# Attention and recurrence served from two queues, chunk 1's norms at a higher rate, output banks copied first

## The chip, the cores and the metric

The kernel runs on one core of a Trainium2 chip. The metric is the device time of one launch in microseconds (us), median of several runs. TensorE (PE) does the products, VectorE (DVE), ScalarE (ACT) and GpSimd (POOL) the rest, and SyncE (SP) issues the DMA transfers from one queue, in order.

## The reference

One layer of a decoder trunk on 1024 prompt rows and 64 sample rows (8 sequences of 8), 1024 wide:

```python
x = x + 0.5 * rms_norm(swiglu(rms_norm(x, norm_ffn1_pre), ffn1_w_gu, ffn1_w_down), norm_ffn1_post)
h = rms_norm(x, norm_mix_pre)
z = h @ w_in + b_in
q, k, v, hq, hf, hi, hg = jnp.split(z, ...)
a = rms_norm(window_attention(q, k, v, attn_sinks), attn_out_norm)   # 128 back, learned sinks
f = lb + (1 - lb) * sigmoid(hf)
o, S = hgrn2_chunked(silu(hq), 1 - f, log(f), hi, s0)                # gated linear recurrence
o = rms_norm(o, hg_out_norm) * silu(hg)
x = x + rms_norm(concat([a, o]) @ w_out, norm_mix_post)
x = x + 0.5 * rms_norm(swiglu(rms_norm(x, norm_ffn2_pre), ffn2_w_gu, ffn2_w_down), norm_ffn2_post)
```

The feed-forward layers are 2816 wide inside. Keys, values and states are returned too.

## The kernel before

**Chunks.** The rows are cut into three chunks: chunk 0 has two blocks of 128 prompt rows and the 64 sample rows (320 columns), chunks 1 and 2 have three blocks each (384 columns). Every fp32 matrix is split into a high and a low part (`split`, L254 to L256: ACT casts the high part, DVE or POOL subtracts it for the low one), and every product is done as three (`mm3`, L276 to L280). The feed-forward layers treat chunk 0 plainly (`up0`, `down`) and chunks 1 and 2 together by seven products of sums of halves; the down part of that is `pair` (L925), whose argument names products by key, as (5,3), (7,), (4,). A product of `pair` takes eleven 128-row slices in six groups (five of two slices, one of one). For each group SP loads the weights (`raw<-fb`, L880) and the activations (`ar<-fa`, L892, into a slot of the tag h384, 8 slots), and they are split; the activations are fetched one group ahead. The products go to three PSUM banks, which `put` (L901) adds to the sums after the last group (L905).

**The middle of the layer** (L1573 to L1603) is where the change is. In program order: `w_in_units(0)`, the projection of chunk 0; products (5,3), (7,) and (4,) of the first feed-forward layer, which belong to chunks 1 and 2; `w_in_units(1)`; `w_out_units(0)`; `w_in_units(2)`; the first five units of the second feed-forward layer for chunk 0 (`f2.head`, each unit two banks of 24 products); `w_out_units(1)`; nine more units; `w_out_units(2)`. For chunks 1 and 2 `w_out_units` is done twice, for each half of the columns, in three banks of 128x512.

**Side work.** Small work is written as generators and woven into the products. `stream(name, gen, rate)` (L95) enters one; each `tick()` (L98), called once to twice per weight tile, advances every stream by its rate in steps; `need(name)` (L108) runs what is left of one to its end there. Streams of norms are `half`, `c0`, `c1` and `c2`: `half_n` (L407) squares a half and multiplies it by the gain, `post_n` (L416) loads the residual (`xt`, L424), adds it (L426) and stores the sum (`x1N`, L427), `pre_n` (L430) scales, transposes on TensorE (L454), and splits (L459) into the tiles `h` that `w_in_units` reads. `done1` and `half1` enter these at the rate `RA1` = 0.75, `done_mix` at `RB0` and `RB1`. The stream `m0`, `m1` or `m2` is the mixer of a chunk: `mixer(n)` (L1449) alternates one step of attention (`attn_block`, L1110, ten steps a block) with one of the recurrence (`hgrn_block`, L1265, twelve steps a block). For chunk 0 it has sample attention (L1299), the output of keys and values, and the sample recurrence (L1378) as well. It is entered when all of the chunk's projection is written, and drained by `need` ahead of the chunk's `w_out`.

Within a recurrence block, `intra` (L1184) makes a 64-row causal product by halving: at each level TensorE does small products `lv` (L1204) or `l` (L1228), after which DVE and POOL multiply their operands for the next one (L1239, L1241). In attention, `sc` are the scores, `pT` the transposed weights (L1165), `pv` the weighted values (L1176).

The order of the instructions on each engine is fixed when the program is built, by a scheduler that weighs readiness against program order. Each engine then works through its own row and waits at an instruction whose operands aren't there. Slots of a pool (`t2` 8, `h384` 8, `big` 12, `wsp` 8, `raw` 3, PSUM `mm` 4 and `ax` 4) tie a later request to the last reader of an earlier one.

**Output banks.** At the end of a half of `w_out_units(1)` and `(2)`, ACT squares each of the three banks for the norm (L1495), and DVE multiplies it by the gain into SBUF (L1496). The bank is free after both.

Of the kernel before, what the change touches and what calls it, by code (L numbers as in the profile page):

```python
# [13 lines left out]
AF = mybir.ActivationFunctionType  # L14
# [29 lines left out]
def tile_step(ctx: ExitStack, tc: tile.TileContext, A: dict, O: list):  # L44
# [53 lines left out]
    def tick():  # L98
        for name in list(streams):
            st = streams[name]  # L100
            st[2] += st[1]
            while st[2] >= 1.0:
                st[2] -= 1.0
                if next(st[0], "end") == "end":
                    del streams[name]
                    break

    def need(name):  # L108
# [860 lines left out]
    def mixing(tp, h):  # L969
# [27 lines left out]

        def w_in_units(n):
            w = WIDTH[n]
# [31 lines left out]
            for m in range(1, 4):  # L1031
                tr(m, z["q"][:, m, :w])
            z["k"] = big()
            for a in range(4):
# [400 lines left out]

        def both(*gens):
            gens = list(gens)
            while gens:
                for g_ in list(gens):
                    if next(g_, "end") == "end":  # L1440
                        gens.remove(g_)
                    else:
                        yield

        def chain(*gens):
            for g_ in gens:
                yield from g_

        def mixer(n):  # L1449
            MT[n] = new_h(n)  # L1450
            at = [attn_block(n, b) for b in range(NPB[n])]
            hg = [hgrn_block(n, b) for b in range(NPB[n])]
            if n == 0:
                at = at + [sample_attn(), kv_out(0)]
                hg = hg + [sample_hgrn()]
            if n == 2:
                at.append(kv_out(2))
            yield from both(chain(*hg), chain(*at))
            if n == 2:
                nc.sync.dma_start(O[4][0, 0].rearrange("h k v -> k h v"), state[0])  # L1460

# [9 lines left out]
        def w_out_units(n, ys, sums):  # L1471
# [14 lines left out]
            for hf in range(2):  # L1486
# [7 lines left out]
                for i in range(3):  # L1494
                    S.activation(junk, banks[i], AF.Square, accum_out=sm[:, 0, 4 * hf + i:4 * hf + i + 1])  # L1495
                    V.tensor_tensor(y[hf][:, i], banks[i], g, op=ALU.mult)  # L1496

        return w_in_units, mixer, w_out_units


# [3 lines left out]

    RM = [0.95, 1.0, 1.3]
    RA0, RA1, RB0, RB1 = 1.2, 0.75, 0.6, 0.8
    HEAD1, HEAD2 = 6, (5, 14, 22)
# [64 lines left out]

    with tc.tile_pool(name="mx", bufs=1) as tp:  # L1573
        w_in_units, mixer, w_out_units = mixing(tp, hmix)
        need("c0")
        w_in_units(0)
        stream("m0", mixer(0), RM[0])
        half1(1)
# [120 lines left out]
```

## Time and profile before

| | us |
|---|---|
| median of 3 runs | 2049.44 |
| lowest, highest | 2048.64, 2050.24 |
| span of the profiled execution | 2045.3 |
| TensorE busy in it | 2006.7 |

The profiled execution's own time beside its span isn't given apart from the three runs; the median is 4.1 us above the span. A row of the windows view gives, for one stretch of the span, the busy time and the count of instructions on each engine, then the clock that TensorE was granted (1.00 is full). A row of the timeline gives start, duration, engine, line, operation, tiles and shape, and in brackets the idle time before it with what ended it.

### The profile page before, as it was taken

The numbers are of one execution on the slowest core, as the hardware profiler recorded it, in microseconds if no ns is written. First come the engines' busy times: TensorE is split into PE (matmuls) and PEld (weight loads), VectorE is DVE, ScalarE is ACT, GpSimd is POOL, SyncE is SP. The second block draws the span as 40 slices with busy tenths as digits, with TensorE's granted clock in tenths as the row PEclk, the third lists the DMA queues.
The fourth block names the chain that finished last, engine by engine and source line by source line (L and its number), as shares of the span: only waits on it lengthen the run. The fifth ranks groups of instructions, "written<-read, shape, count | busy, mean of one in ns | idle before, by whom it ended". The sixth has DMA issues, their size and how long they took to land.

```text
span 2045.3 us, 34828 instructions
## 1 busy us (share of the span) xinstructions
PE 2006.7 (98%) x13273; PEld 1856.7 (91%) x13273; DVE 1452.6 (71%) x2493; ACT 933.5 (46%) x1679; POOL 550.1 (27%) x508
## 2 busy tenths in 40 slices
PE   9999999999999999899999998999999999999998
PEld 8999999999998987697898897878999999999886
DVE  5776667885568557777678756766889888655667
ACT  6534333444455445435344444544544444444552
POOL 0013433654113101311113310210046554510201
PEclk9999999999999999799999998999999999999999
DMA  8455445556777545556434243525565556576874
GB/s 254 140 158 169 139 156 164 200 182 219 238 235 213 159 149 171 160 145 184 127 96 138 87 141 94 163 87 184 168 193 200 191 188 209 195 241 222 289 257 136
DMA packets 372368, 360.09 MB, mean 176 GB/s; under 512 B 40590, under 2 KB 294361, under 8 KB 372185
## 3 DMA queue, kind: packets, MB, share of 16 engines
q1 hardware_dynamic: 371401, 356.42, 55.2%
q8 instruction: 104, 1.70, 0.3%
q10 hardware_dynamic: 800, 1.44, 0.2%
q14 instruction: 63, 0.52, 0.1%
HBM read 279.85 MB, written 78.94 MB: 175 GB/s over the span
## 4 chain that ended last, share of the span: by engine, by line
PE 91%; DVE 3%; DMA 3%; ACT 1%; issue 1%; SPq 0%; DVEq 0%; ACTq 0%
PE mm L278 27%; PE mm L279 26%; PE mm L280 26%; PE c L280 1%; PE c L278 1%; PE c L279 1%; PE sc L1127 1%; DMA ar<-fa 1%; PE pv L1176 1%; DMA raw<-in_ffn_w_gu_dram 1%; PE lv L1204 1%; PE pT L1165 1%; PE tr L497 1%; DVE w L256 1%; DMA xt<-in_x_prompt_dram 0%
## 5 line engine op out<-in xcount | busy, mean ns | idle before, releaser
L278 PE MATMUL mm<-h,wsph 128*128 128x320 f32 (+1 forms) x1296 | 414.7, 322 | 3.7 <-ACT sg L632 2.2
L279 PE MATMUL mm<-h,wsph 128*128 128x320 f32 (+1 forms) x1296 | 412.5, 319 | 0.0
L280 PE MATMUL mm<-h,wspl 128*128 128x320 f32 (+1 forms) x1296 | 411.7, 318 | 0.0
L255 ACT CAST wsph<-raw 128x1024 fp32r<-128x1024 f32 x202 | 211.3, 1048 | 293.9 <-PE mm L279 237.1
L256 DVE TENSOR_TENSOR wspl<-raw,wsph 128x1024 fp32r<-128x1024 f32 x202 | 251.0, 1245 | 119.3 <-ACT wsph L255 118.5
L256 DVE TENSOR_TENSOR w<-raw,w 128x512 fp32r<-128x512 f32 (+1 forms) x226 | 250.0, 1110 | 84.9 <-ACT w L255 82.8
L255 ACT CAST w<-raw 128x512 fp32r<-128x512 f32 (+1 forms) x226 | 169.6, 754 | 207.3 <-PE mm L279 109.8
L278 PEld LDWEIGHTS mm<-h,wsph 128*128 128x128 f32 x1296 | 244.6, 189 | 11.0 <-issue 3.1
L280 PEld LDWEIGHTS mm<-h,wspl 128*128 128x128 f32 x1296 | 244.7, 189 | 4.0 <-issue 3.5
L279 PEld LDWEIGHTS mm<-h,wsph 128*128 128x128 f32 x1296 | 245.0, 189 | 3.2 <-issue 2.6
L278 PE MATMUL mm<-h,w 128*128 128x384 f32 x704 | 235.8, 335 | 1.2 <-DVE big L725 1.2
L279 PE MATMUL mm<-h,w 128*128 128x384 f32 x704 | 235.8, 335 | 0.0
L280 PE MATMUL mm<-h,w 128*128 128x384 f32 x704 | 230.5, 335 | 0.0
L279 PE MATMUL mm<-w,h 128*128 128x512 f32 x462 | 181.6, 393 | 0.0
L278 PE MATMUL mm<-w,h 128*128 128x512 f32 x462 | 180.8, 395 | 0.5 <-DVE big L905 0.5
L280 PE MATMUL mm<-w,h 128*128 128x512 f32 x462 | 179.5, 392 | 0.0
L280 PE MATMUL mm<-big,w 128*128 128x384 f32 x528 | 176.8, 335 | 1.5 <-DVE w L256 1.5
L279 PE MATMUL mm<-big,w 128*128 128x384 f32 x528 | 176.7, 335 | 0.0
L278 PE MATMUL mm<-big,w 128*128 128x384 f32 x528 | 176.6, 335 | 0.0
L709 POOL TENSOR_TENSOR big<-big 128x384 f32<-128x384 f32 x88 | 111.7, 1269 | 236.5 <-ACT big L722 116.2
L256 DVE TENSOR_TENSOR w<-t,w 128x512 fp32r<-128x512 f32 x176 | 160.5, 922 | 17.5 <-ACT w L255 17.0
L278 PEld LDWEIGHTS mm<-h,w 128*128 128x128 f32 x704 | 132.2, 188 | 1.6 <-DVE big L725 1.6
(359 smaller groups left out, 3881.2 us busy)
## 6 DMA issues: line engine op xcount, KB each, us to landing
raw<-in_ffn_w_gu_dram SPq DMA_DIRECT2D x156, 512.0 KB
raw<-in_ffn_w_down_dram SPq DMA_DIRECT2D x74, 512.0 KB
raw<-in_w_in_dram SPq DMA_DIRECT2D x54, 512.0 KB
ar<-fa SPq DMA_DIRECT2D x70, 384.0 KB
big<-in_ffn_w_down_dram SPq DMA_DIRECT2D x88, 256.0 KB
fb<-big SPq DMA_DIRECT2D x44, 512.0 KB
raw<-fb SPq DMA_DIRECT2D x40, 512.0 KB
fa<-big SPq DMA_DIRECT2D x22, 768.0 KB
```

The source lines that it names most:

```text
L255: S.copy(hi, src)
L256: (lo_eng or V).tensor_tensor(lo, src, hi.bitcast(F32), op=ALU.subtract)
L278: PE.matmul(out, a[0], b[0], start=first, stop=False, skip_group_check=resume)
L279: PE.matmul(out, a[0], b[1], start=False, stop=False, skip_group_check=resume)
L280: PE.matmul(out, a[1], b[0], start=False, stop=last, skip_group_check=resume)
L497: PE.transpose(bank[:, i * P:(i + 1) * P], y[kh][:, i, k * P:(k + 1) * P], ident)
L709: G.tensor_tensor(e[:, i], e[:, i], e[:, i + 1], op=ALU.mult)
L1127: PE.matmul(banks[g][:, i * 256:i * 256 + wk], zq[64 * g:64 * g + 64, 2 * pr + i, b * P:(b + 1) * P], kx[64 * g:64 * g + 64, k0:k0 + wk], ...
L1165: PE.transpose(bank[:, (i * nk + kb) * P:(i * nk + kb + 1) * P], pt[g][:, i, kb * P:(kb + 1) * P], ident)
L1176: PE.matmul(ob[64 * g:64 * g + 64, pr * 256:pr * 256 + 256], vn[:, vb, g * 64:g * 64 + 64], pT[g][:, :2 * wk].rearrange("p (i k t) -> p k ...
L1204: PE.matmul(b4[cs, a, :32], x[:, a, cs], y[:, a, cs], start=True, stop=True)
```

## The change

1. `mixer`, `both` and `chain` go. Two queues, `at` (attention) and `hg` (recurrence), are entered as streams that never end ahead of `w_in_units(0)`, at 0.45 and 0.65 steps a tick. In each `w_in_units(n)`, `ready("at", n)` appends the chunk's attention blocks when the queries are projected, and `ready("hg", n)` its recurrence blocks when the recurrence's values are. Before, the whole mixer waited for the end of the projection, and advanced 0.95, 1.0 and 1.3 steps a tick for chunks 0, 1 and 2.
2. Ahead of `w_out_units(n)`, `need_mix(n)` runs what is left of chunks up to n, one step of each queue in turn.
3. `RA1`, the rate of `half`, `c1` and `c2`, goes from 0.75 to 1.2.
4. In `w_out_units`, ACT copies the three banks to SBUF first; then ACT squares the copies, and POOL multiplies them by the gain.

```diff
+    queues = {"at": [], "hg": []}
+
+    def steps(name):
+        q = queues[name]
+        while True:
+            while q:
+                if next(q[0][1], "end") == "end":
+                    q.pop(0)
+                else:
+                    break
+            yield
+
+    def need_mix(n):
+        gens = {k: streams[k][0] for k in queues}
+        while any(q and q[0][0] <= n for q in queues.values()):
+            for k, q in queues.items():
+                if q and q[0][0] <= n:
+                    next(gens[k])
...
             for m in range(1, 4):
                 tr(m, z["q"][:, m, :w])
+            ready("at", n)
...
                 V.tensor_tensor(hv[:r, i], banks[i][:r], bhi[:r], op=ALU.add)
+            ready("hg", n)
...
-        def mixer(n):
-            MT[n] = new_h(n)
-            at = [attn_block(n, b) for b in range(NPB[n])]
-            hg = [hgrn_block(n, b) for b in range(NPB[n])]
-            if n == 0:
-                at = at + [sample_attn(), kv_out(0)]
-                hg = hg + [sample_hgrn()]
-            if n == 2:
-                at.append(kv_out(2))
-            yield from both(chain(*hg), chain(*at))
...
+        def ready(kind, n):
+            if n not in MT:
+                MT[n] = new_h(n)
+            if kind == "at":
+                gens = [attn_block(n, b) for b in range(NPB[n])]
+                if n == 0:
+                    gens += [sample_attn(), kv_out(0)]
+                if n == 2:
+                    gens.append(kv_out(2))
+            else:
+                gens = [hgrn_block(n, b) for b in range(NPB[n])]
+                if n == 0:
+                    gens.append(sample_hgrn())
+                if n == 2:
+                    gens.append(state_out())
+            queues[kind] += [(n, g) for g in gens]
...
                 for i in range(3):
-                    S.activation(junk, banks[i], AF.Square, accum_out=sm[:, 0, 4 * hf + i:4 * hf + i + 1])
-                    V.tensor_tensor(y[hf][:, i], banks[i], g, op=ALU.mult)
+                    S.copy(y[hf][:, i], banks[i])
+                for i in range(3):
+                    S.activation(junk, y[hf][:, i], AF.Square, accum_out=sm[:, 0, 4 * hf + i:4 * hf + i + 1])
+                    G.tensor_tensor(y[hf][:, i], y[hf][:, i], g, op=ALU.mult)
...
-    RM = [0.95, 1.0, 1.3]
-    RA0, RA1, RB0, RB1 = 1.2, 0.75, 0.6, 0.8
+    RAT, RHG = 0.45, 0.65
+    RA0, RA1, RB0, RB1 = 1.2, 1.2, 0.6, 0.8
...
         need("c0")
+        stream("at", steps("at"), RAT)
+        stream("hg", steps("hg"), RHG)
         w_in_units(0)
-        stream("m0", mixer(0), RM[0])
         half1(1)
...
         w_in_units(1)
-        need("m0")
-        stream("m1", mixer(1), RM[1])
+        need_mix(0)
         w_out_units(0, ym, sums)
...
         f2.head(range(HEAD2[0]))
-        need("m1")
-        stream("m2", mixer(2), RM[2])
+        need_mix(1)
         w_out_units(1, ym, sums)
...
-        need("m2")
+        need_mix(2)
+        streams.pop("at"), streams.pop("hg")
         w_out_units(2, ym, sums)
```

Two places show how the order of the instructions moves. Line numbers of the changed kernel are 19 to 21 higher.

**The loads of key (4,).** This is SP's row before, from the third of the six activation loads (`ar<-fa`) on. The other names are the weights of the product (`raw<-fb`), chunk 1's gain row (`gb`), residual (`xt`) and sums (`x1N`), and weights of the next projection.

```order
L892 DMA ar_8348<-fa_114 128x2x384
L880 DMA raw_8275<-fb_115 128x2x512
L892 DMA ar_8398<-fa_114 128x2x384
L880 DMA raw_8341<-fb_115 128x2x512
L892 DMA ar_8451<-fa_114 128x2x384
L880 DMA raw_8391<-fb_115 128x2x512
L400 DMA gb_7894<-in_norm_ffn_post_dram 128x512
L880 DMA raw_8444<-fb_115 128x512
L424 DMA xt_8092<-in_x_prompt_dram 128x512
L424 DMA xt_8096<-in_x_prompt_dram 128x512
L262 DMA raw_8661<-in_w_in_dram 128x8x128
L427 DMA x1N_96<-big_5759 128x512
```

Five of the six loads stand ahead of chunk 1's norm, the sixth behind it. And this is SP's row of the changed kernel, from the last stores of that norm on; `osc` is an output of sample attention.

```order
L446 DMA x1N_96<-big_5759 128x512
L443 DMA xt_8421<-in_x_prompt_dram 128x512
L446 DMA x1N_96<-big_6059 128x512
L443 DMA xt_8425<-in_x_prompt_dram 128x512
L446 DMA x1N_96<-big_5759 128x512
L446 DMA x1N_96<-big_6059 128x512
L1388 DMA osc<-t_1207_8540 128x64
L911 DMA ar_8636<-fa_114 128x2x384
L419 DMA gb_8688<-in_norm_ffn_post_dram 128x512
L911 DMA ar_8722<-fa_114 128x2x384
L911 DMA ar_8778<-fa_114 128x2x384
```

`ar_8636` is the second load; the first, `ar_8556`, stands 28 rows ahead of it and ahead of the norm. So the second to sixth loads are behind the norm now. On DVE, 80 rows stand between the eviction of key (7,)'s last bank (`big_6060<-mm_8193`, L924) and the split of `ar_8636`. On TensorE, 116 small products stand between the first group and the second, whose first product is the last row here; `tr` are the transposes of chunk 1's norm, `sav` and `spT` parts of the sample work.

```order
L473 MATMUL tr_8673<-ident,big_5759 128x128
L473 MATMUL tr_8679<-ident,big_5759 128x128 x3
L1423 MATMUL sav_8602<-big_6991,At_8397 32x128 x2
L1427 MATMUL sav_8602<-big_8603,t_1221_8605 32x128 x8
L1423 MATMUL sav_8602<-big_6991,At_8397 32x128 x2
L473 MATMUL tr_8702<-ident,big_6059 128x128 x3
L473 MATMUL tr_8708<-ident,big_6059 128x128 x3
L1372 MATMUL spT_8744<-ident,t_1239_8663 128x128
L1373 MATMUL spT_8744<-ident,t_1239_8663 8x128
L297 MATMUL mm_8626<-w_8551,h_8635 128x512
```

Chunk 1's transposes and the sample work, which were behind the fifth group of key (4,) or in the next projection, stand ahead of its second group.

**The start of `f2.head`.** This is TensorE's row before, at the passage from the second unit (last bank `mm_12055`) to the third (`mm_12157`).

```order
L278 MATMUL mm_12055<-h_11456,wsph_11955 128x320
L279 MATMUL mm_12055<-h_11458,wsph_11955 128x320
L280 MATMUL mm_12055<-h_11456,wspl_11956 128x320
L1290 MATMUL u_12074<-big_9554,t_1735_12029 128x128 x4
L278 MATMUL mm_12157<-h_11455,wsph_12008 128x320
L279 MATMUL mm_12157<-h_11457,wsph_12008 128x320
```

Only one small group stands between the units. In the changed kernel the four banks of the first two units (`mm_12270`, `mm_12271`, `mm_12413`, `mm_12414`) get their last products in turn, and between their end and the third unit (`mm_12520`) stand sixteen products `lv_12135`, four of attention's scores, and then:

```order
L1121 MATMUL ms_11994<-t_1731_11969,ones 128x128
L1225 MATMUL lv_12190<-t_1738_12022,t_1739_12023 32x32 x16
L1225 MATMUL lv_12248<-t_1738_12022,t_1739_12023 32x32 x16
L1225 MATMUL lv_12308<-t_1738_12022,t_1739_12023 32x32 x16
L1186 MATMUL pT_12344<-ident,t_1759_12176 128x128 x2
L1186 MATMUL pT_12351<-ident,t_1760_12179 128x128 x2
L1249 MATMUL l_1790_12378<-t_1738_12022,t_1739_12023 32x32 x8
L1186 MATMUL pT_12344<-ident,t_1759_12176 128x128 x2
L1186 MATMUL pT_12351<-ident,t_1760_12179 128x128 x2
L1249 MATMUL l_1791_12403<-t_1738_12022,t_1739_12023 64x64 x4
L1197 MATMUL pv_12433<-t_1783_12349,vn_10694 64x256
L297 MATMUL mm_12520<-h_11799,wsph_12362 128x320
```

The levels of one recurrence block of chunk 1 and a part of its attention stand ahead of the third unit now.

More of the change, by code (lines that the diff above doesn't have):

```diff
@@ L996, in col_tile, with w_in_units @@
             return load_up(w_in, c * P)
-        def w_in_units(n):
+        def w_in_units(n, ready):
             w = WIDTH[n]
@@ L1434, in kv_out, with state_out @@
             yield
[L1436 to L1447, printed above, removed]
-        def mixer(n):
-            MT[n] = new_h(n)
-            at = [attn_block(n, b) for b in range(NPB[n])]
-            hg = [hgrn_block(n, b) for b in range(NPB[n])]
-            if n == 0:
-                at = at + [sample_attn(), kv_out(0)]
-                hg = hg + [sample_hgrn()]
-            if n == 2:
-                at.append(kv_out(2))
-            yield from both(chain(*hg), chain(*at))
-            if n == 2:
-                nc.sync.dma_start(O[4][0, 0].rearrange("h k v -> k h v"), state[0])
+        def ready(kind, n):
[14 more added lines that the diff above has]
+            queues[kind] += [(n, g) for g in gens]
+        def state_out():
+            nc.sync.dma_start(O[4][0, 0].rearrange("h k v -> k h v"), state[0])
+            yield
         def w_out_rows(k0, k1, c0, c1):
@@ L1494, in w_out_units @@
                 for i in range(3):
-                    S.activation(junk, banks[i], AF.Square, accum_out=sm[:, 0, 4 * hf + i:4 * hf + i + 1])
-                    V.tensor_tensor(y[hf][:, i], banks[i], g, op=ALU.mult)
-        return w_in_units, mixer, w_out_units
+                    S.copy(y[hf][:, i], banks[i])
+                for i in range(3):
+                    S.activation(junk, y[hf][:, i], AF.Square, accum_out=sm[:, 0, 4 * hf + i:4 * hf + i + 1])
+                    G.tensor_tensor(y[hf][:, i], y[hf][:, i], g, op=ALU.mult)
+        return lambda n: w_in_units(n, ready), w_out_units
     def seq(*gens):
@@ L1573, in tile_step @@
     with tc.tile_pool(name="mx", bufs=1) as tp:
-        w_in_units, mixer, w_out_units = mixing(tp, hmix)
+        w_in_units, w_out_units = mixing(tp, hmix)
         need("c0")
+        stream("at", steps("at"), RAT)
+        stream("hg", steps("hg"), RHG)
         w_in_units(0)
-        stream("m0", mixer(0), RM[0])
         half1(1)
```

## The prediction

> **What bounds the kernel now.** I read the page's busy shares first, then the mean product time in the timeline, then the stretches in which TensorE loses time, then who was waited for in them.
>
> ```profile
> span 2045.3 us, 34828 instructions
> ## 1 busy us (share of the span) xinstructions
> PE 2006.7 (98%) x13273; PEld 1856.7 (91%) x13273; DVE 1452.6 (71%) x2493; ACT 933.5 (46%) x1679; POOL 550.1 (27%) x508
> PE 91%; DVE 3%; DMA 3%; ACT 1%; issue 1%; SPq 0%; DVEq 0%; ACTq 0%
> ```
>
> TensorE is busy for 2006.7 of 2045.3 us and holds 91% of the chain that ended last. The change keeps its products, so it can only win or lose in the few stretches where TensorE waits or runs at a slower granted clock. These are the ones that it touches, in the windows view (length, then busy time and count of PE, PEld, DVE, ACT, POOL, then granted clock, DMA share, GB/s):
>
> ```profile
> core 0: us, PE busy (x) PEld busy (x) DVE busy (x) ACT busy (x) POOL busy (x), PEclk, DMA share, GB/s
> 844.40:862.30 17.90, 11.66 (x121) 8.15 (x119) 14.20 (x42) 10.71 (x25) 4.90 (x8) 0.58 0.70 181
> 862.30:871.00 8.70, 6.65 (x25) 5.25 (x25) 4.62 (x13) 2.73 (x5) 0.00 (x0) 0.68 0.12 32
> 1235.00:1243.00 8.00, 5.78 (x98) 4.21 (x97) 6.62 (x23) 4.06 (x15) 3.15 (x7) 0.81 0.03 12
> 1262.00:1275.00 13.00, 9.83 (x47) 8.15 (x46) 10.46 (x46) 3.87 (x18) 0.52 (x1) 0.74 0.39 121
> 1338.00:1346.00 8.00, 6.69 (x77) 5.68 (x76) 4.95 (x9) 4.36 (x6) 3.44 (x7) 1.00 0.48 154
> 1346.00:1363.00 17.00, 13.79 (x160) 10.81 (x158) 12.17 (x28) 9.35 (x17) 2.46 (x3) 0.80 0.26 73
> 1380.00:1401.00 21.00, 18.12 (x96) 13.72 (x94) 9.26 (x26) 7.37 (x19) 0.86 (x1) 1.00 0.39 118
> 1100.00:1120.00 20.00, 20.00 (x129) 17.15 (x127) 17.63 (x58) 8.29 (x15) 4.98 (x6) 1.00 0.35 105
> ```
>
> I call the first two rows place A: the end of the down product of key (4,). The next five are the drains: what is left of a mixer is run to its end ahead of, or within, w_out(1) (1235 to 1275) and w_out(2) (1338 to 1401). The last row is the end of w_in(2), just ahead of f2.head: TensorE loses nothing there, but VectorE is already busy for 17.63 of 20 us.
>
> **What the change removes.** The two queues are further on when each w_out begins: counted in ticks, nothing of a mixer is left for need_mix to drain, and the last mixer ends some 20 ticks ahead of w_out(2). So the drains go. Their idle time is length less busy: 2.22 + 3.17 + 1.31 + 3.21 + 2.88 = 12.8 us. Their slow clock is busy time by (1 − clock): 5.78 × 0.19 + 9.83 × 0.26 + 13.79 × 0.20 = 6.4 us. Together **−19.2 us**.
>
> **What it moves into place A.** The waits of the timeline (idle time in brackets, with who ended it) show what that place is made of today.
>
> ```profile
> 843.95 0.39 PE L278 MATMUL mm<-w,h 128*128 128x512 f32 x1
> 844.18 0.39 PE L279 MATMUL mm<-w,h 128*128 128x512 f32 x1
> 846.29 0.46 PE L1204 MATMUL lv<-t,t 128*32 128x32 f32 x32 [1.50 <-DVE sm L1149]
> 848.65 1.97 PE L1165 MATMUL pT<-ident,t 128*128 128x128 f32 x8 [1.90 <-DVE t L1158]
> 852.32 0.66 PE L1204 MATMUL lv<-t,t 128*32 128x32 f32 x32 [1.70 <-DVE sm L247]
> 855.14 1.97 PE L1176 MATMUL pv<-t,vn 128*64 128x256 f32 x6 [1.11 <-DVE t L1168]
> 864.81 1.09 PE L1277 MATMUL kT<-ident,t 128*128 128x128 f32 x4 [1.86 <-DVE h L459]
> ```
>
> The last 512-wide product before the gap starts at 844.40. Then the engine does small mixer products with a wait on VectorE between them, because the sixth and last group of key (4,) isn't there yet. SP's queue says why:
>
> ```profile
> 806.84 0.46 SPq L892 DMA_DIRECT2D ar<-fa  x1
> 813.07 0.36 SPq L892 DMA_DIRECT2D ar<-fa  x1
> 817.97 0.46 SPq L400 DMA_DIRECT2D gb<-in_norm_ffn_post_dram  x1
> 830.41 3.33 SPq L427 DMA_DIRECT2D x1N<-big  x2
> 845.41 3.05 SPq L427 DMA_DIRECT2D x1N<-big  x3
> 856.15 0.42 SPq L892 DMA_DIRECT2D ar<-fa  x1
> ```
>
> Five of the six activation loads go out up to 813.07. The sixth stands behind chunk 1's norm: its gain row (817.97), and the six stores of x1N, the last at 845.41 or later, each of which waits for VectorE. It goes out at 856.15. In the changed order, one load is ahead of that norm and **five are behind it**. The second group of key (4,) therefore waits for VectorE to work through chunk 1's norm and what the queues have put between: 80 rows from the eviction of key (7,)'s last bank to the split of the second load.
>
> Today's cost, as above: idle 6.24 + 2.05, slow clock 11.66 × 0.42 + 6.65 × 0.32, together 15.3 us. The new cost: in today's gap a VectorE row takes 14.20 / 42 = 0.338 us and the engine is busy for 14.20 / 17.90 = 0.79 of the time, so 80 rows take 80 × 0.338 / 0.79 = 34.1 us. In them TensorE has the first group, 18 products at 0.23 (two starts above) = 4.1, and 116 small products at 5.78 / 98 = 0.059 (the row at 1235) = 6.8. That leaves 23.2 us idle. I add 2.1 us for the restart (today's second row, 6.65 × 0.32) and 2 us, an estimate, for groups three to six, whose loads start late as well: 27.3, so **+12.0**. Bounds: VectorE without a pause at 6.62 / 23 = 0.288 a row gives 23.0 − 10.9 = 12.1 (−3 against today). If the small products, at half the clock, only lengthen VectorE's waits instead of filling them, 34.1 − 4.1 + 2.1 + 4 = 36 (+21). I take the middle, nearest to today's own gap.
>
> The Trainium skill has a rule on the clock: by its page "TensorE: Matmul & The Clock Gate", section "What's actually happening", the slow clock comes after an idle window of about 3.4 us. Here the longest single wait in place A is 1.90 us and the granted clock is 0.58, so the rows differ from that, and they decide; by the rule the restart would come only after longer gaps than today's, and the sum would be 2 us less if there were none.
>
> **What it moves into f2.head, place E.** In the order before, the ten banks of head's five units have their products each in a row, with a few small ones between. In the changed order those of the first two units come with their second halves interleaved, and ahead of the third unit TensorE has a chain of chunk 1's mixer work: eight small groups (lv, ms, lv, lv, lv, then pT, l, l) and pv, nine hand-overs, most of which need VectorE or POOL to finish the group before. TensorE runs in order, so the third unit waits behind them. The five waits quoted for place A are 1.50, 1.90, 1.70, 1.11 and 1.86, on average 1.61: 9 × 1.61 = 14.5 us. Some of them pass beside each other, since attention and recurrence are two chains, so I take **+12**, with 0 as the lower bound (all under the interleaved products) and 9 × 1.90 = 17 as the upper. VectorE at 17.63 of 20 us in the stretch ahead is why I don't take the lower.
>
> **What else moves.** In w_in(0) and the products of keys (5,3) and (7,) mixer steps come earlier. They are the same steps, and TensorE has a product to issue at each tick: 0, bounds −2 and +2. The bank copies:
>
> ```profile
> L1496 DVE TENSOR_TENSOR big<-mm,gb 128x512 f32<-128x512 f32 x12 | 7.9, 683 | 3.3 <-DMA gb<-in_norm_mix_post_dram 2.5 <-ACT junk L1495 0.7
> L1495 ACT ACTIVATE junk<-mm 128x512 bf16<-128x512 f32 x12 | 7.2, 598 | 10.0 <-PE mm L280 10.0
> L908 ACT COPY big<-mm 128x512 f32<-128x512 f32 x6 | 3.4, 579 | 0.0
> L1634 POOL TENSOR_TENSOR big<-big,gb 128x512 f32<-128x512 f32 x3 | 3.8, 1297 | 0.0
> L921 POOL TENSOR_TENSOR big<-big,big 128x512 f32<-128x512 f32 x6 | 10.1, 1702 | 97.8 <-DVE big L905 97.8
> ```
>
> VectorE loses 12 multiplies of 0.683 (8.2 us), ACT gains 12 copies of 0.579 (6.9), POOL gains 12 multiplies of 1.297 to 1.702 (15.6 to 20.4). A bank is free after a copy instead of after a square and a multiply: the 683 ns and the wait for the gain row leave the release. ACT and POOL are busy for 46% and 27%, so both hide it: 0. If the cover is gone, each half of w_out gives its norm three POOL multiplies later, 3.9 to 5.1 us.
>
> **The sum.** 2045.3 − 19.2 + 12.0 + 12.0 = 2050.1 us of span. The median before, 2049.44, lies 4.1 us above the profiled span, which I add: **2054.2 us**. A measurement of this kernel tells some 0.2% from no change, 4.1 us: faster is below 2045.3, slower above 2053.5.
>
> **The rivals.**
>
> 1. *Place E costs nothing, and the change is faster.* The chain ahead of the third unit is over while the interleaved products of the first two units still run. For it: TensorE is busy for all 20 us of that row today, with mixer work between. Against it: the order puts the chain behind those products, and VectorE has little room. Price −12: 2042.2. It ends below 2045.3 as soon as TensorE waits less than 3 us there and place A is as forecast.
> 2. *Place A runs at VectorE's own pace.* Its rows are ready, and the pauses of today vanish: −15 against my term, 2039. It decides when the gap is under 18 us. For it: some 40 rows of the 80 are short steps on one column of numbers. Against it: those are a chain too, and VectorE paused for 21% of today's gap.
> 3. *Both stalls come, at half their size* against my terms: 2048, no change that can be told. The time is moved from the drains to A and E.
> 4. *POOL's multiplies slow VectorE.* A VectorE row with two inputs in SBUF takes longer beside POOL, as the minimum, median and maximum here show:
>
> ```profile
> L1239 DVE TENSOR_TENSOR t<-t,t x4: 409/414/825, 1236.2 to 1252.3; 128x256 f32<-128x256 f32 x4
> ```
>
> Twelve multiplies that each cost VectorE 0.41 (825 − 414) are 5 us, that each block it throughout 12 × 1.30 = 16. With half of the latter in TensorE's path: 2062. Against it: VectorE isn't what bounds w_out once the drains are gone. The Trainium skill's "SBUF — State Buffer", section "Who interferes with whom", says that a VectorE instruction with two SBUF inputs and a POOL instruction that reads SBUF exclude each other for a whole instruction, which speaks against this edit; the 825 agrees with it.
> 5. *The change doesn't do what it says*: something is left to drain. Then −19.2 is missing, 2073. The tick counts speak against it.
>
> **Chances.** Forecast as above 0.42, rival 1 0.24, rival 2 0.12, rival 3 0.12, rival 4 0.07, rival 5 0.03. Slower by over 0.2%: 0.46 (0.36 of the forecast's own spread, rivals 4 and 5). Within 0.2%: 0.25 (0.06 of the forecast, 0.07 of rival 1, rival 3). Faster: 0.29 (the rest of rival 1, and rival 2). The range is 2036 to 2067: below, A at its bound (−15) with E three less than my term; above, A at +21 (9 more than mine) with E at some 4 more. Both bounds at once, on either side, and rival 5 are left out. Since both signs hold much of the chance, the forecast's own range stands beside it: 2050 to 2060.
>
> **What would show it.** In the changed profile: the drains' waits (on the pT, lv and sg rows, and on the w_out bank's multiply) gone from around both w_out stages, at a clock near 1. Between the first and second group of key (4,): a gap of some 30 us between 512-wide products, about 7 us of it small ones, with a clock near 0.6, and the second ar<-fa issued only after the stores of x1N. Ahead of head's third unit: nine waits of 1 to 2 us on VectorE or POOL. Wrong if the second load goes out before those stores, if TensorE doesn't wait in head, or if the time turns up in w_in(0) or the earlier products.

## The result and the profile after

The changed kernel takes 2060.86 us (median of 4 runs, 2059.99 to 2062.11) against 2049.6 us beside it: ratio 1.0057, 95% interval 1.0043 to 1.0072. It is slower by 11 us, about half a percent. The forecast was slower, 2054.2 us, with a range of 2036 to 2067.

The page of the changed kernel, in the lines that answer to those shown of the one before:

```profile
span 2059.1 us, 34830 instructions
...
PE 1998.7 (97%) x13273; PEld 1853.9 (90%) x13273; DVE 1450.2 (70%) x2481; ACT 946.4 (46%) x1695; POOL 557.2 (27%) x520
...
PE 88%; DVE 4%; DMA 3%; ACT 2%; issue 2%; POOL 0%; DVEq 0%; ACTq 0%; POOLq 0%; SPq 0%
```

The same 13273 instructions of TensorE, and TensorE's share of the chain down from 91% to 88%. The span is 13.8 us longer. Where, the windows by stage tell. First the kernel before: products (5,3) to (4,), the five units of head, w_out(1), the nine units of head, w_out(2) (length, then busy time and count of PE, PEld, DVE, ACT and POOL, clock, DMA share, GB/s):

```profile
734.60:862.30 127.70, 120.53 (x950) 93.11 (x948) 91.49 (x224) 65.06 (x138) 25.05 (x33) 0.94 0.57 169
...
1166.40:1209.90 43.50, 43.50 (x380) 42.33 (x379) 28.17 (x66) 18.65 (x32) 8.82 (x15) 1.00 0.44 125
1209.90:1254.40 44.50, 42.28 (x361) 33.40 (x360) 23.91 (x49) 19.86 (x44) 6.29 (x11) 0.96 0.32 97
1254.40:1371.80 117.40, 109.71 (x1062) 96.43 (x1062) 85.50 (x240) 62.14 (x130) 22.14 (x34) 0.94 0.42 128
1371.80:1414.80 43.00, 40.09 (x206) 31.65 (x205) 21.88 (x46) 15.49 (x35) 2.37 (x5) 1.00 0.44 130
```

And the same stages of the changed kernel:

```profile
746.20:908.20 162.00, 134.59 (x1064) 102.05 (x1063) 111.34 (x259) 67.55 (x137) 33.66 (x44) 0.89 0.52 153
...
1192.20:1265.80 73.60, 63.32 (x671) 55.07 (x670) 46.99 (x127) 34.23 (x67) 18.81 (x32) 0.86 0.29 86
1265.80:1310.50 44.70, 44.70 (x324) 34.99 (x323) 29.77 (x70) 21.43 (x48) 11.54 (x17) 1.00 0.33 98
1310.50:1396.10 85.60, 81.91 (x740) 77.98 (x739) 59.93 (x131) 43.56 (x83) 12.75 (x18) 0.98 0.56 172
1396.10:1428.80 32.70, 32.70 (x146) 27.07 (x145) 10.54 (x9) 14.59 (x22) 5.02 (x4) 1.00 0.61 164
```

The lengths alone mislead, since mixer work has moved between the stages; idle time (length less busy) and clock don't. Around both w_out, TensorE's idle time falls from 2.22 + 7.69 + 2.91 = 12.8 us to 3.7. In the products it rises from 7.2 (9.2 with the sixth group of key (4,), which runs behind 862.30) to 27.4, and in the five units of head from nothing to 10.3.

To compare all runs I add up, by stage, **lost time**: for each instruction of TensorE, the time from its start to the next one's, less the median of that for its line and shape. It holds waits and slow clock alike. What is left, the sum of the medians, is 1959 to 1969 us in every run; lost time and medians together are 10.6 to 11.1 us short of the span. Where a group has an even count, the upper of its two middle values is taken. With their mean the figures of the stage "products and w_in(1)" are 1.4 to 8.5 us higher, as the small groups of the sample work lie there, and those of the other stages up to 3.1 us. So in that stage a difference of a few us between two runs says little.

| stage | before | after | forecast of the difference |
|---|---|---|---|
| up to the products | 7.2 | 9.4 | 0 |
| products and w_in(1) (place A) | 24.7 | 38.4 | +12.0 |
| w_out(0), w_in(2) | 9.7 | 9.5 | 0 |
| five units of head (place E) | 0.4 | 18.3 | +12.0 |
| w_out(1), nine units, w_out(2) (the drains) | 28.4 | 9.4 | −19.2 |
| rest | 3.2 | 3.6 | 0 |
| all | 73.6 | 88.6 | +4.8 |

**Place A** in TensorE's timeline of the changed kernel, between the first and the second group of key (4,) (rows with a wait over 2 us, and the first product of the second group):

```profile
849.65 1.08 PE L1280 MATMUL hT<-ident,t 128*128 128x128 f32 x4 [6.89 <-DVE t L1276]
...
854.87 0.47 PE L1372 MATMUL spT<-ident,t 128*128 128x128 f32 x1 [2.96 <-ACT t L1367]
...
866.19 0.44 PE L1380 MATMUL spv<-kv,t 128*32 128x64 f32 x8 [8.41 <-issue]
...
873.25 0.69 PE L473 MATMUL tr<-ident,big 128*128 128x128 f32 x2 [4.48 <-DVE big L465]
...
882.08 0.48 PE L297 MATMUL mm<-w,h 128*128 128x512 f32 x1
```

SP's queue beside it:

```profile
809.02 0.39 SPq L911 DMA_DIRECT2D ar<-fa  x1
...
841.40 0.35 SPq L419 DMA_DIRECT2D gb<-in_norm_ffn_post_dram  x1
...
844.04 0.90 SPq L443 DMA_DIRECT2D xt<-in_x_prompt_dram  x2
...
865.79 1.55 SPq L446 DMA_DIRECT2D x1N<-big  x2
...
868.39 0.93 SPq L911 DMA_DIRECT2D ar<-fa  x1
...
880.71 8.30 SPq L911 DMA_DIRECT2D ar<-fa  x3
```

The second load goes out at 868.39, behind the norm's stores, as the order had said, and the second group starts at 882.08. The norm's gain row comes at 841.40; before, it was at 817.97. For the longest wait, 8.41 us, the profile names no releaser ("issue"). Its operand `t` is the transposed sample weights, which VectorE copies at 865.79 and 866.00 (L1375, L1376), just behind residual additions of the norm (L445) that waited 2.33 and 2.97 us for their rows `xt`.

**Place E**, ahead of the third unit of head:

```profile
1213.12 0.66 PE L1225 MATMUL lv<-t,t 128*32 128x32 f32 x32 [1.67 <-DVE t L1260]
...
1218.20 0.80 PE L1121 MATMUL ms<-t,ones 128*128 128x128 f32 x2 [0.76 <-DVE t L1119]
...
1222.57 0.66 PE L1225 MATMUL lv<-t,t 128*32 128x32 f32 x32 [2.41 <-DVE t L1260]
...
1224.45 0.66 PE L1225 MATMUL lv<-t,t 128*32 128x32 f32 x32 [1.23 <-DVE t L1260]
...
1228.11 1.11 PE L1186 MATMUL pT<-ident,t 128*128 128x128 f32 x4 [3.00 <-DVE t L1179]
...
1232.99 0.56 PE L297 MATMUL mm<-h,wsph 128*128 128x320 f32 x1
```

The windows view of the two places, as in the stages:

```profile
842.40:882.10 39.70, 14.76 (x167) 9.78 (x159) 23.96 (x78) 14.15 (x43) 6.17 (x10) 0.57 0.47 147
...
1211.20:1233.00 21.80, 11.52 (x175) 8.02 (x173) 14.96 (x48) 9.36 (x22) 7.08 (x11) 0.54 0.34 98
```

No product of head runs in the 21.8 us of the second row; TensorE has 11.52 us of small work, at a clock of 0.54, and 10.3 us of waits, seven in all.

### The profile page after: what moved, and what is told of

Read it like the earlier page. It is cut to its first block, busy times and chain, and to the rows that moved or that the text cites. A ratio compares the mean times of both kernels' runs of the same rounds, so it can differ in the third digit from the quotient of the medians.

```text
span 2059.1 us, 34830 instructions
## 1 busy us (share of the span) xinstructions
PE 1998.7 (97%) x13273; PEld 1853.9 (90%) x13273; DVE 1450.2 (70%) x2481; ACT 946.4 (46%) x1695; POOL 557.2 (27%) x520
## 4 chain that ended last, share of the span: by engine, by line
PE 88%; DVE 4%; DMA 3%; ACT 2%; issue 2%; POOL 0%; DVEq 0%; ACTq 0%; POOLq 0%; SPq 0%
PE mm L297 26%; PE mm L299 26%; PE mm L298 26%; PE c L299 1%; PE c L297 1%; PE c L298 1%; PE pv L1197 1%; DMA raw<-in_ffn_w_gu_dram 1%; DMA ar<-fa 1%; PE sc L1148 1%; PE pT L1186 1%; PE lv L1225 1%; PE tr L516 1%; DMA ar<-act 0%; DVE wspl L275 0%
## 5 line engine op out<-in xcount | busy, mean ns | idle before, releaser
L275 DVE TENSOR_TENSOR w<-raw,w 128x512 fp32r<-128x512 f32 (+1 forms) x226 | 244.9, 1088 | 88.9 <-ACT w L274 87.2
```

Source lines behind the costliest of these rows:

```text
L275: (lo_eng or V).tensor_tensor(lo, src, hi.bitcast(F32), op=ALU.subtract)
```

## The experiments

Ratios are against the kernel before, run again beside each edit (medians of 2048.38 to 2049.60 us). All runs' lost time by stage, for reference (columns as the rows of the table above, then the sum; us):

```
before                      7.2   24.7    9.7    0.4   28.4    3.2    73.6
after                       9.4   38.4    9.5   18.3    9.4    3.6    88.6
e1_before_ra1               3.4   34.3   12.2    0.4   26.2    4.0    80.5
e2_hold                     3.5   37.2    9.0   18.6    9.7    3.8    81.8
e3_before_banks             8.0   27.2   10.2    0.4   18.9    5.2    69.9
e4_rates                    6.5   35.1    3.8    0.9   16.8    3.9    67.0
e5_sample_later             4.7   42.9   11.4   13.0   23.0    4.4    99.4
e6_ra075                    8.2   33.6    7.9   18.7    9.0    5.6    83.0
e7_old_banks                8.0   37.7    8.9   18.6    5.5    4.0    82.7
e8_later_075_rates         10.7   37.6    3.5    4.7   30.6    3.2    90.3
e9_rows_raw                 8.0   38.1    9.6   18.4    9.3    3.5    86.9
e10_before_banks_raw        8.2   16.7   11.0    0.4   17.4    4.2    57.9
e11_rates_raw              10.2   36.3    4.1    1.1   16.8    3.3    71.8
e12_rates_raw_hold          9.7   34.6    4.3    1.1   17.6    4.4    71.7
```

### One edit alone, and the claim that the prediction saw

Chunk 1's higher rate, alone in the kernel before:

```diff
-    RA0, RA1, RB0, RB1 = 1.2, 0.75, 0.6, 0.8
+    RA0, RA1, RB0, RB1 = 1.2, 1.2, 0.6, 0.8
```

> The kernel before with RA1 = 1.2 and nothing else. Theory (the stall in key (4,) comes from the rate of chunk 1's norm alone: it claims its h384 slots ahead of the second activation load, which then waits for the norm): five of the six loads go out behind the norm's stores here as well, a gap of 25 to 35 us between the first and second group of key (4,), less of it sample work, and the old gap at 844 to 871 gone; the drains stay. 2049.6 + 8 to 16, so 2058 to 2066. Rival (the stall comes from the sample work that the queues put there, or is spread over the stages): the rate alone changes little, 2047 to 2053.

2059.85 us, ratio 1.0055 (1.0040 to 1.0071). The time is in the expected range, but not all of it in the expected place. Five loads are behind the norm here too, and the gap between the first and second group is at 826 to 849, yet about as much is lost in it as in the old one at 844 to 870 (16.0 us against 16.1). What came in addition is a wait of 7.71 us ahead of w_out(0), on a transpose of the sample work:

```profile
988.49 0.41 PE L1402 MATMUL sav<-big,At 64*32 64x128 f32 x4
996.61 0.66 PE L1080 MATMUL oT<-ident,t 64*128 64x64 f32 x4 [7.71 <-DMA raw<-in_w_out_dram]
```

The row puts it down to a weight load, but the operand `t` is written by VectorE just before:

```profile
996.03 0.48 DVE L1076 TENSOR_SCALAR t<-t,sm 64x512 f32<-64x512 f32 x1 [0.25 <-DMA raw<-in_w_out_dram]
```

That row ends the norm of sample attention, which begins at 993.34 on ScalarE after a wait of 2.03 us for the sample output read back from memory (`t<-osc`). So it is the last of chunk 0's mixer that is drained here, one step after the other. In the kernel before nothing of the kind stands there.

The claim by itself: in the changed kernel, the norm waits nine steps longer before it claims its four h384 slots.

```diff
         yield
         yield
+        if n == 1:
+            for _ in range(9):
+                yield
         h[n] = new_h(n)
```

> The changed kernel, where chunk 1's norm lets nine more steps pass before it claims the slots of its result; rates, queues and banks stay as changed. Theory (the claim): five loads are ahead of the norm again, the gap between the first and second group of key (4,) is under 3 us, and what is left is a wait at the start of the next projection, about as in the kernel before (15 us): 2060.9 - 16 = 2045, at most 2050. Rival 1 (the norm is only moved, and the whole wait comes at the projection): 2058 to 2062. Rival 2 (VectorE is too full with sample work there, whoever claims first): the gap in key (4,) stays above 15 us, 2055 to 2062.

2063.18 us (ratio 1.0071, 1.0056 to 1.0086): no gain, rival 1, a little above its range. All groups but the last of key (4,) run without a gap, and the wait stands at the start of w_in(1) instead:

```profile
835.00:860.00 25.00, 24.27 (x139) 19.60 (x138) 19.26 (x44) 7.70 (x20) 7.12 (x5) 1.00 0.44 111
860.00:905.00 45.00, 22.91 (x218) 12.59 (x216) 27.00 (x76) 13.85 (x35) 12.06 (x15) 0.62 0.55 162
```

22 us of idle time in the second row: here the loads' place in SP's queue decides where the wait falls, and not how long it is (37.2 us lost in the stage, against 38.4).

Bringing the rate back in the changed kernel does much the same:

```diff
-    RA0, RA1, RB0, RB1 = 1.2, 1.2, 0.6, 0.8
+    RA0, RA1, RB0, RB1 = 1.2, 0.75, 0.6, 0.8
```

> The changed kernel with RA1 back at 0.75; queues and banks as changed. New theory: as with the claim held back, five loads are ahead, but the sample work and the norm still meet, now at the start of the next projection (110 small products there in the order): 2057 to 2064, no gain. Rival (RA1 is what costs, as alone in the kernel before, where it cost 11 us): 2047 to 2052.

2062.01 us (1.0070, 1.0053 to 1.0086): no gain, as the theory had it. But the wait stands ahead of the sixth group of key (4,), from 860 to 902, as it does in the kernel before. Lost in products and w_in(1): 33.6, against 24.7 before with neither edit (27.2 with the banks copied), 34.3 with the rate alone, 38.4 with both. Each of the two costs some 9 us there, and together they cost 14, not 18.

### The banks

```diff
                 for i in range(3):
-                    S.activation(junk, banks[i], AF.Square, ...)
-                    V.tensor_tensor(y[hf][:, i], banks[i], g, op=ALU.mult)
+                    S.copy(y[hf][:, i], banks[i])
+                for i in range(3):
+                    S.activation(junk, y[hf][:, i], AF.Square, ...)
+                    G.tensor_tensor(y[hf][:, i], y[hf][:, i], g, op=ALU.mult)
```

Alone in the kernel before:

> The kernel before with the three copies first, squares and POOL multiplies behind them, and nothing else. Theory (hidden but for the bank release): the 2.6 us of waits on the multiply of the banks go, 2046 to 2050. Rival (POOL's multiplies hold up VectorE or the norm behind w_out): 2053 to 2062.

2039.83 us, ratio 0.9955 (0.9940 to 0.9970): faster than either range, and than both kernels. w_out(1) takes 40.2 us instead of 44.5 and w_out(2) 38.7 instead of 43.0, both without idle time. The 2.6 us of waits on the banks' multiplies were only part of the 9.5 us that the stage of the drains gained (28.4 to 18.9). The order behind the earlier release changed as well; that this gave the rest isn't shown.

Taken back in the changed kernel:

> The changed kernel with the old end of w_out: squares and VectorE multiplies from the banks. Theory (the 9 us that the copies bring to the kernel before come from w_out meeting the drains; where nothing is drained they bring little): 2060 to 2064. Rival (they bring the same here): 2068 to 2071.

2056.85 us (1.0037, 1.0024 to 1.0050): the old end of w_out is 4 us *faster* there, which neither had. The two intervals overlap a little (the changed kernel has 1.0043 to 1.0072), so 4 us is near the least that these runs can tell. There is nothing at the w_out stages to gain: both kernels lose nothing in w_out(2). The difference is in the nine units of head, where POOL's row of the changed kernel has the three multiplies of the second half ahead of a step of chunk 2's recurrence:

```profile
1323.43 0.74 POOL L1262 TENSOR_TENSOR t<-t,t 128x256 f32<-128x256 f32 x1 [3.83 <-PE lv L1225]
1329.01 0.67 POOL L1262 TENSOR_TENSOR t<-t,t 128x256 f32<-128x256 f32 x1 [4.84 <-PE lv L1225]
1329.64 4.43 POOL L1514 TENSOR_TENSOR big<-big,gb 128x512 f32<-128x512 f32 x3
1334.02 1.10 POOL L1262 TENSOR_TENSOR t<-t,t 128x256 f32<-128x256 f32 x1
...
1345.29 0.79 POOL L1262 TENSOR_TENSOR t<-t,t 128x256 f32<-128x256 f32 x1 [0.88 <-PE l L1249]
```

With the old end the last step of that block is done eight microseconds earlier:

```profile
1327.96 0.63 POOL L1262 TENSOR_TENSOR t<-t,t 128x256 f32<-128x256 f32 x1 [3.76 <-PE lv L1225]
...
1337.61 0.62 POOL L1262 TENSOR_TENSOR t<-t,t 128x256 f32<-128x256 f32 x1 [3.44 <-PE l L1249]
```

TensorE waits 2.22 us for `l` and 0.73 for `kT` on L1262 at 1344 to 1346 in the changed kernel. That fits 3.5 to 4 us. VectorE is held up by the same multiplies, the first half's at 1302.28 to 1306.00 and the second half's at 1329.64 to 1334.07:

```profile
1301.99 0.16 DVE L267 TENSOR_TENSOR sm<-sm 128x4 f32<-128x4 f32 x1
1303.60 1.19 DVE L267 TENSOR_TENSOR sm<-sm 128x4 f32<-128x4 f32 x1
1331.26 3.35 DVE L445 SCALAR_TENSOR_TENSOR big<-big,sm,xt 128x512 f32<-128x512 f32 x2
```

The same small row takes 0.16 us alone and 1.19 beside a multiply. The two residual additions take 3.35 us, where one takes 0.75 (the median of the 24 that ran while POOL was idle). VectorE's half of the delayed step (L1260) ends at 1335.40, POOL's at 1335.12. So the step is late on both engines, and how much of the 4 us is owed to each is read from the rows, not tried by itself.

### The chain in head

```diff
-    RAT, RHG = 0.45, 0.65
+    RAT, RHG = 0.4, 0.6
```

> The changed kernel with the queues at 0.40 and 0.60 steps a tick in place of 0.45 and 0.65. Theory (the second stall is a matter of which mixer steps fall on the passage from the second to the third unit of head): the chain ahead of the third unit is gone from the order, so its 15 us are gone, while the stall in key (4,) stays: 2060.9 - 12 to 16 = 2045 to 2049. Rival (steps that don't run there are owed: they drain ahead of w_out(1) or w_out(2) as in the kernel before): 2055 to 2063.

2043.64 us (ratio 0.9979, 0.9968 to 0.9990), 17 us less than the changed kernel and a little under the theory's range. The five units of head lose nothing:

```profile
1186.10:1234.30 48.20, 48.20 (x499) 45.53 (x499) 34.96 (x86) 25.71 (x50) 9.88 (x18) 1.00 0.43 124
1277.70:1378.60 100.90, 89.97 (x787) 83.62 (x786) 74.56 (x184) 50.24 (x104) 18.07 (x24) 0.95 0.47 142
```

Part of it is owed, as the rival said: the nine units lose 16.8 with w_out (9.4 at the higher rates). But 17.4 is won in head and 6 in w_out(0) and w_in(2); the 3 us at place A are too few to read. So place E hung on which mixer step falls on the passage between two units.

### What makes place A long

Two theories followed. The first: sample work and norm meet. Sample attention and the sample recurrence are queued with chunk 1's blocks:

```diff
                 gens = [attn_block(n, b) for b in range(NPB[n])]
-                if n == 0:
-                    gens += [sample_attn(), kv_out(0)]
+                if n == 1:
+                    queues[kind] += [(0, sample_attn()), (0, kv_out(0))]
...
                 gens = [hgrn_block(n, b) for b in range(NPB[n])]
-                if n == 0:
-                    gens.append(sample_hgrn())
+                if n == 1:
+                    queues[kind].append((0, sample_hgrn()))
```

> The changed kernel, with sample attention and the sample recurrence put into the queues with chunk 1's blocks and not with chunk 0's; rates as changed. New theory (it isn't the order of the loads but the meeting of the sample work with chunk 1's norm on VectorE and in the t2 slots that makes the stall long): 44 small products instead of 116 stand ahead of the second group of key (4,), the stall there falls from about 30 us to 12 to 18, and the total to 2060.9 - 15 = 2046, or down to 2036 where the changed step count also shortens the chain in head (the order has 36 small products there, not 90). Rival (the norm alone sets that stall, whatever runs beside it): the stall stays at 27 to 31, 2055 to 2061.

2078.66 us (1.0153, 1.0132 to 1.0174). It fails, and comes out above both ranges: the stall at key (4,) does get shorter (24 us lost there, against 33), but the sample work is then owed ahead of w_out(0), and products and w_in(1) together lose 42.9. What is left of the stall is mostly the norm by itself, whose transposes wait for VectorE's scaling:

```profile
859.29 2.79 PE L473 MATMUL tr<-ident,big 128*128 128x128 f32 x12 [12.77 <-DVE big L465]
```

With the lower rates and RA1 = 0.75 as well:

> Sample work with chunk 1's blocks, RA1 = 0.75, queues at 0.40 and 0.60, banks copied first. New theory (the two stalls are the whole loss): no stall at key (4,) beyond the 14 us of the kernel before, none in head: 2028 to 2038, faster than both. Rival (the sample work only meets something else, in the projections of chunks 1 and 2, or drains ahead of w_out): 2043 to 2055.

2065.10 us (1.0074, 1.0059 to 1.0089): the rival's mechanism, at more than its price (its range ended at 2055). 37.6 in that stage, 30.6 around w_out(1) and w_out(2).

The second: the norm's rows come late because the mixers hold the t2 slots.

```diff
-    def gain_row(ap, scale, hf):
-        g = tmp2("gb")
+    def gain_row(ap, scale, hf, raw=False):
+        g = rawslot((P, 512)) if raw else tmp2("gb")
...
-        g = gain_row(gpost, scale, hf)
+        g = gain_row(gpost, scale, hf, True)
...
-                xt = tmp2("xt")
+                xt = rawslot((P, 512)) if xsrc is xN[0] or xsrc is xN[1] else tmp2("xt")
```

> The changed kernel, with the gain rows of the norms and the residual rows of chunks 1 and 2 after the first feed-forward layer loaded into slots of the tag raw (the weight loads' own) and not of t2, where the mixers keep theirs. Theory (slots of t2: the norm of chunk 1 begins late, its gain row at 841 us and not at 818, because the mixers that now run beside it hold the t2 slots, and its six residual rows come through two slots): gain row before 830, no wait of VectorE on residual rows, the stall at key (4,) 10 to 18 us instead of 30: 2042 to 2050. Rival 1 (VectorE has norm, mixer blocks and sample work to do there in any case, and the slots only order it): stall 24 to 30, 2055 to 2061. Rival 2 (the weight loads, which now share three slots with the norm, come late): waits on the splits of weights, 2061 to 2070.

2061.26 us (1.0060, 1.0045 to 1.0075): no gain. The slots did hold the norm up: in raw slots the gain row comes at 796.94 and the last store at 830.46, 35 us earlier. The second load still goes out only at 862.15, now behind a store of sample attention (`osc`), for which SP waits 4.7 us:

```profile
796.94 0.35 SPq L419 DMA_DIRECT2D raw<-in_norm_ffn_post_dram  x1
...
830.46 0.45 SPq L446 DMA_DIRECT2D x1N<-big  x1
...
861.77 0.34 SPq L1388 DMA_DIRECT2D osc<-t  x1
862.15 1.24 SPq L911 DMA_DIRECT2D ar<-fa  x1
```

Even so the gap is shorter: 22 us are lost between the first and second group, against 33, with 13 idle instead of 25. The stage loses 38.1, as before, because the 11 us are lost again on either side of it, 4 in the products and 7 in w_in(1). There the weights, which share the three raw slots with the norm now, come late at least in part, as rival 2 had it. ScalarE's casts of the products' weights wait 21 us for their loads from 800 to 862, where none waited for a load in the changed kernel, and a product of w_in(1) waits for its split:

```profile
ACT w L274 <- DMA raw<-fb: 21.2, 5, 10.5
922.64 0.45 PE L297 MATMUL mm<-h,wsph 128*128 128x384 f32 x1 [2.21 <-ACT wsph L274]
```

So the time can't tell rival 1 from rival 2, and the rows speak for a part of the theory and for rival 2. Slots that neither the mixers nor the weights use weren't tried. In the kernel before with banks copied first, the same edit does win:

> The kernel before with banks copied first and the norms' rows in raw slots. Theory (slots of t2 also hold up the norm in the kernel before, where its stall at key (4,) is 14 us): 2039.8 - 5 to 12 = 2028 to 2035. Rival (VectorE bounds that stall): 2037 to 2042.

**2029.58 us, ratio 0.9904 (0.9890 to 0.9919): 19 us faster than the kernel before, 31 than the changed one.** It is as the theory had it. The stage loses 16.7 instead of 27.2; at key (4,) little is left of the old gap:

```profile
820.00:862.00 42.00, 38.59 (x359) 28.57 (x349) 37.51 (x91) 23.90 (x51) 17.37 (x21) 0.96 0.46 130
```

The rows in raw slots with the queues at the lower rates, and, second, with the claim held for four steps besides:

> The changed kernel with the queues at 0.40 and 0.60 and the norms' rows in raw slots. Theory of the slots: the stall at key (4,) of 25 us in the run with these rates falls to 10 to 15, 2043.6 - 10 to 15 = 2028 to 2034. Rival (VectorE): 2040 to 2046.

> As the run before it, and chunk 1's norm lets four more steps pass before it claims its result's slots, so that three of the six loads of key (4,) are ahead of it and not one. Theory (with the norm early, the order of the loads decides what is left): another 4 to 10 us less, 2020 to 2030. Rival (what isn't waited for in key (4,) is waited for at the next projection): the same as the run before it, within 3 us.

2046.69 us (0.9989, 0.9978 to 1.0001) and 2048.22 us (0.9999, 0.9990 to 1.0008): neither theory's gain, and both close to their rival's range. The stage loses 36.3 and 34.6 us. In the first of the two the gap shrinks again (23 us lost, against 31 with these rates alone), and w_in(1) loses 9.7 instead of 2.8, now on the end of the sample work.

So with the queues, the stage from the first of these products to w_out(0) loses 34 to 43 us in each of the ten kernels that have them. Taking the sample work or the t2 slots out of the gap did shorten it, and each time the gain was lost again ahead of it or behind it. VectorE isn't full there (111.34 of 162.00 us in the products of the changed kernel). What stays is an account that no run tries by itself: the mixers' chains, the sample work's and the norm's stand in one fixed order on VectorE, on ScalarE and in SP's queue, and each of them stops the others for a product, a cast or a load. Which of these is the longest wasn't settled.

## Why the prediction was right, and where it wasn't

**The drains go: right.** Forecast −19.2, lost time 28.4 to 9.4, −19.0. What is left there is in part new, the 3.6 us at 1340 to 1346.

**Place A: right in place and size, by luck in the size, and wrong in its cause.** Forecast +12.0, measured +13.7 for products and w_in(1). The gap itself is as worked out: 39.7 us from 842.4 to 882.1, with 24.9 idle (23.2 forecast), a clock of 0.57, and the second load behind the norm's stores. But two terms under that idle time were wrong and offset each other. VectorE's stretch from the eviction at 835.65 to the split at 879.75 took 44.1 us, not 34.1, with 84 rows between the two, not 80: in the gap the engine was busy for 23.96 of the 39.7 us (60%, not 79%), with shorter rows than forecast (0.307 us against 0.338) and waits on the residual rows of 5.3 us, which the sum didn't have. And the small products took 14.76 us in the gap, not 6.8. The 116 are counted in the program, while their price of 0.059 is that of an instruction in the trace, and the trace has 196 instructions between the first and the second group. (A level `lv` has sixteen products in the program's row of head and 32 in the timeline.) The slow clock did the rest.

The prediction made the load's place the cause. With five loads ahead of the norm again about as much is lost (37.2 us with the claim held, 33.6 with RA1 back, against 38.4), at the start of w_in(1) or ahead of the sixth group. The step that failed is "the second group therefore waits": it does, but in the two orders tried what was put before the norm only moved the wait.

**Place E: right, too small.** Forecast +12, measured +17.9. The bound above had 17. The waits are fewer and shorter than forecast: seven with 10.3 us together, 1.47 on average, where nine with 14.5 were cut down to 12. The term that the sum left out is the slow clock: 11.52 us of work at 0.54, by the prediction's own way of counting 11.52 × 0.46 = 5.3 us. The chain, its lines and the unit that it holds up are those of the forecast, and the run with lower rates, whose order lacks it, has the stage without loss. One reading was wrong: the row 1100 to 1120 lies in the middle of w_in(2), not at its end, which is at 1166; that VectorE is full ahead of head doesn't follow from it.

**The banks: forecast 0, and not 0.** They are worth 9 us to the kernel before and cost the changed one 4. Rival 4 had VectorE slowed by POOL's multiplies, and the rows show that (1.19 us instead of 0.16, 3.35 instead of 1.5). They show POOL's own queue as well, which the prediction didn't have: a recurrence step stands behind three multiplies of 1.48 us each. At most 4 of the 8 us of rival 4's price are seen.

The rate of chunk 1's norm was costed only through the order of the loads. It costs 11 us alone in the kernel before, 7 of them at a place that the prediction doesn't name, and nothing in the changed kernel. The direction was right because the two named stalls, +31.6 together, are more than the drains; the size was 6.7 us too small, six of them in head, and the time lies just outside the narrower range of 2050 to 2060. The wide range held a gain as well as a loss, so that the time fell into it says little. Ahead of the products 2.2 us more are lost, at the edge of the ±2 around the forecast 0. Rival 3 was added up wrongly: half of both +12 is 12 us less, 2042 and not 2048.

## What to carry to other kernels

A wait that a change removes ahead of one stage is often owed at the next: count it there before it is booked as a gain, and look for what else needs the same result. What lies beside an edit decides its sign: the same bank copies won 9 us where drains met w_out and lost 4 where a recurrence step needed POOL and VectorE beside them, and the same raw slots won 10 us in one kernel and were paid back in late weights in another. A count taken from the program must not be priced by the instruction of a trace before one checks that both count the same. Try each part of such a change alone: one part of this one, with the norm's rows out of the mixers' slots, gives the best kernel of the study.

## What the runs showed of the hardware

The granted clock falls without any long wait. At place A of the kernel before it is 0.58 over 17.9 us in which no single wait of TensorE is over 1.90 us, while only 11.66 us are busy; at place E it is 0.54 with none over 3.00. In both it falls behind a few us that are thinly filled: from 844.0 to 847.4 in the kernel before TensorE is busy for 1.25 of 3.4 us at a clock of 1.00, and the next 3.4 us have 0.50; from 1209.4 to 1212.8 in the changed kernel it is busy for 2.05 of 3.4 us at 1.00, and the next 3.4 us have 0.51. How thinly is enough wasn't measured.

A POOL multiply of 128x512 can stretch a VectorE row beside it to its own length, however small the row is: 128x4 elements took 1.19 us beside a multiply of 1.27, and 0.16 alone.
